# Input projections of the second token half in two 512-column chunks, with split weights reloaded from DRAM

## The chip, the cores and the metric

The kernel runs on one core of one Trainium2 chip. The metric is the device time of one execution in microseconds (us), as the median of several executions. Beside the timed executions one execution was profiled.

## The reference

One layer of a hybrid decoder. A token row is normalised, multiplied by one wide matrix, and its columns go to three branches; the branches are concatenated, multiplied by an output matrix, normalised and added to the input.

```python
xn = rmsnorm(x, g_pre)
proj = xn @ w_in                      # 1024 -> 4864 columns
a_c, b_c, g_c, x_r, g_r, q, g_q = jnp.split(proj, ...)   # 768 x5, 512 x2
u = a_c * sigmoid(b_c)
c = silu(layernorm(depthwise_causal(u, conv_w, conv_b))) * silu(g_c)   # 31 taps
xc = depthwise_causal(x_r, lru_conv_w, lru_conv_b)                     # 4 taps
h = linear_recurrence(a, bx_t, h0)    # a, bx_t from two small gate products of xc
rr = h * silu(g_r)
o = attention(q, mem_k, mem_v) * silu(g_q)              # 4 heads, 256 memory rows
y = x + rmsnorm(concatenate([c, rr, o]) @ w_out, g_post)
```

There are 2048 prompt tokens and 32 sample tokens (8 requests of 4) with caches of their own.

## The kernel before

Everything is float32. A product of two float32 matrices is made of three matmuls in a faster number format (`mm3`, L103): each operand is split into a high part that this format holds and the low rest, and high by high, high by low and low by high are added up in PSUM. `split` (L108) makes the two parts: ScalarE copies the high part (L109) and VectorE subtracts it from the source (L110).

**Two parts, then a phase 2.** In phase 1 the tokens are on the columns. Part 0 holds tokens 0 to 1023 and the 32 sample tokens, part 1 tokens 1024 to 2047; below they are called the first and the second part. Each part makes 38 projections, one per 128 output columns of `w_in` (six each for A, B, the conv gate GC, XR and GR, four each for Q and GQ). A projection (`proj`) loads its weight tile of 512 KB by a transfer on SyncE's queue (SP), splits it into `wh` and `wl`, and runs over the tokens in three chunks of 352, 352 and 320 columns (the last has 32 sample columns more in the first part); each chunk takes 8 contraction tiles of three matmuls. `wh`, `wl` have two buffers. The normalised x of a chunk stands in the tiles `xh`, `xl`, three buffers of 352 columns. In the second part x is loaded transposed and split by `split_cols` (ScalarE L356, VectorE L357).

Behind a projection stands an evacuation: for the conv gate a copy to `kc` and a store to DRAM (`store_mix`, L401), for A a ScalarE copy times 0.5 (L429) and a VectorE product, for GQ a silu. In `attn_o` the attention output is copied by ScalarE (L722) and multiplied by the gate on VectorE.

**What sets the order.** The string `ORDER` lists for each part which steps run when, with counts of chunks (G glu, X LRU input, S LRU scan, O LRU output, C conv gate, q and o attention); Tile's scheduler turns it into one instruction list for each engine. Every engine runs its list in order, and a transfer is issued by the engine on whose queue it stands: weight, x and cache loads on SP, all stores of phase 1 (`st_`) and a few reloads (`kv`, L663) on GpSimd (POOL). POOL also runs the `pow` of the norms and the three casts of each LRU gate chunk (L561 to L563, from `prep`), which wait for a VectorE split.

**Phase 2** multiplies blocks of 128 tokens by `w_out` in matmuls of 512 columns, after loading what phase 1 stored (`cr`, `mr`, L867 and L868).

Of the kernel before, what the change touches and what calls it, by code (L numbers as in the profile page):

```python
# [8 lines left out]
F32 = mybir.dt.float32  # L9
# [7 lines left out]
P = 128  # L17
# [15 lines left out]
EPS = 1e-6  # L33
CW = 352
CONV_LOW = 3000
MIX_HIGH = 500
# [3 lines left out]
NLC = 7  # L40
NCK = 5
NKC = 2
# [5 lines left out]
    "G0 N M1 X0:3 M0 X0:3 M2 X0:3 L X0 G1 G2:3 V G2 S0:2 S0:1 M3 S0:1 S0 C0 O0 C1 q0:3 G3:1 q0 G3 o0 R X1:7 X1 S1:1 G4 S1:1 S1:1 C2 C4 S1 O1 q1:3 G5:1 q1 G5:2 o1 G5 q3:3 C3:1 q3 C3 q2:3 o3:1 q2 o3 o2 C5",  # L48
    "G0:1 G0 s0 s1 p v0 X0 v1 G1 S0:1 G2:1 S0:1 G2 S0:1 S0 C0 O0 q0:3 G3:1 q0 G3:1 o0 G3 G4:3 X1 S1:1 G4 S1:1 S1 C1 O1 q1:3 G5:1 q1 G5 o1 q3:3 q2:1 q3 q2:2 o3:1 q2 o3 o2 C5 C4 C2 C3",
)  # L50
# [18 lines left out]
def hybrid_mixer_kernel(ctx, tc, x, xT, mem, consts, lnc, ccT, lcT, ckT, cv, w_in,  # L69
# [8 lines left out]
    convd = dram.tile([P, NT, TOK], F32, name="convd")  # L78
    rsd = dram.tile([1, TOK], F32, name="rsd")
    kvd = dram.tile([HEADS, P, 8, P], F32R, name="kvd")  # L80

# [13 lines left out]
    def bank(pl, w=512):  # L95
        t = pl.tile([P, 512], F32, tag="b", name="bk")
        return t[:, :w]
# [5 lines left out]
    def mm3(ps, lh, ll, rh, rl, first, last):  # L103
        pe.matmul(ps, lh, rh, start=first, stop=False)  # L104
        pe.matmul(ps, lh, rl, start=False, stop=False)  # L105
        pe.matmul(ps, ll, rh, start=False, stop=last)  # L106

    def split(hi, lo, src):  # L108
        act.activation(hi, src, AF.Copy)  # L109
        dve.tensor_tensor(lo, src, hi.bitcast(F32), op=ALU.subtract)  # L110

# [5 lines left out]
    def phase1():  # L117
        def pl_(name, bufs):
            return ctx1.enter_context(tc.tile_pool(name=name, bufs=bufs))
# [21 lines left out]
        def xslot(dt=F32):  # L141
            return pr.tile([P, XRW], dt, tag="xr", name="xr")
# [92 lines left out]

        def load_w(src, ahead=None):
            with tc.high_priority(offset=W_HIGH if ahead is None else ahead):
                raw = pw.tile([P, KD, P], F32, tag="wr", name="wr", bufs=WR)
                sp.dma_start(raw, src)
                wh = pw.tile([P, KD, P], F32R, tag="wh", name="wh")  # L240
                wl = pw.tile([P, KD, P], F32R, tag="wl", name="wl")
                split(wh, wl, raw)
            return wh, wl
# [53 lines left out]
        for part in range(2):  # L297
            chunks = []
            for c0 in range(0, PART, CW):
                n = min(CW, PART - c0)  # L300
                chunks.append((c0, n, SAMP if part == 0 and n < CW else 0))
            part_chunks.append(chunks)

        def pieces(part, c, r, w):
# [55 lines left out]
        for part in range(2):  # L360
            t0 = part * PART
            has_s = part == 0
            chunks = part_chunks[part]

            xh, xl = [], []
# [5 lines left out]
            ready[FIRST] = load_w(w_in[FIRST], 0)  # L371
            for c, (c0, n, ns) in enumerate(chunks):
                h = px.tile([P, KD, CW], F32R, tag="xh", name="xh")
                l = px.tile([P, KD, CW], F32R, tag="xl", name="xl")
                w = n + ns
                hi, lo = (lambda k: h[:, k, :w]), (lambda k: l[:, k, :w])
                if has_s:
                    if c + 1 < len(chunks):
                        rows[c + 1] = chunk_rows(0, c + 1)
                    if c == 0:  # L380
                        ready[M_A] = load_w(w_in[M_A], 0)
# [4 lines left out]
                xh.append(h)  # L386
                xl.append(l)
            def proj(m, evac):
                wh, wl = ready.pop(m) if m in ready else load_w(w_in[m])
                for c, (c0, n, ns) in enumerate(chunks):  # L390
                    w = n + ns
                    ps = bank(ps_p, w)
# [15 lines left out]
            def glu(i):  # L408
# [113 lines left out]
            def lru_scan(g):  # L522
# [13 lines left out]
                def prep(c):  # L536
                    c0, n, ns = chunks[c]
                    w = n + ns
# [30 lines left out]
                yield  # L569
                for c, (c0, n, ns) in enumerate(chunks):  # L570
                    w = n + ns
# [28 lines left out]
                    for i in range(3):  # L600
# [6 lines left out]
                        if ns:  # L607
# [5 lines left out]
                            dve.tensor_copy(xrb[i][1][:, :, :NS], hv)  # L613
                    if c + 1 < len(chunks):
                        nxt = prep(c + 1)
# [78 lines left out]
            def attn_o(h):  # L694
                kv, probs = att.pop(h)
                sg = {}

                def ev_g(c, ps):
                    c0, n, ns = chunks[c]
                    t = ck()  # L700
                    silu2(t[:, :n + ns], ps)
                    if ns:
                        act.activation(sgq[:, h, :], t[:, n:n + ns], AF.Copy)
                    sg[c] = t

                yield from proj(M_GQ + h, ev_g)
                ot = xslot()
                for q4 in range(2):
# [14 lines left out]
                for c, (c0, n, ns) in enumerate(chunks):  # L723
                    dve.scalar_tensor_tensor(ot[:, c0:c0 + n], ot[:, c0:c0 + n], 0.5, sg[c][:, :n],
                                             op0=ALU.mult, op1=ALU.mult)
                st_.dma_start(mixd[:, 2 * NT + h, t0:t0 + PART], ot[:, :PART])
# [63 lines left out]
            def conv_gate(i):  # L790
                def ev(c, ps):
                    c0, n, ns = chunks[c]
                    t = pk.tile([P, CW], F32, tag="kc", name="kc", bufs=NKC)[:, :n + ns]
# [266 lines left out]
```

## Time and profile before

| | us |
|---|---|
| median of 3 runs | 1429.61 (1429.36 to 1431.13) |
| profiled execution, its own time | 1426.34 |
| span in that profile, first to last instruction | 1424.6 |
| TensorE (PE) busy in the span | 1405.8 (99%) |
| VectorE (DVE) busy | 1096.5 (77%) |
| ScalarE (ACT) busy | 681.3 (48%) |
| GpSimd (POOL) busy | 152.0 (11%) |

The mean granted clock of TensorE is 0.997 of full speed. The span is 1.7 us shorter than the profiled execution's own time. The durations of one matmul overlap with the next, so the price of a matmul is the distance from its start to the next start, and not its own duration. In the profile PEld is TensorE's weight load, which overlaps PE. Idle time stands in the profile with what ended it.

### The profile page before, as it was taken

The page shows a single profiled execution, that of the slowest core. Times are in us where ns is not written, and L with a number is a line of the kernel's source. Part 1 is how long each engine was busy: PE and PEld are TensorE (multiplying, and loading weights), DVE is VectorE, ACT ScalarE, POOL GpSimd, SP SyncE. Part 2 cuts the span into 40 slices and gives each one's busy share as a digit, 9 for nine tenths or more (in the row PEclk, how much of TensorE's full clock was granted, in tenths as well). Part 3 has the DMA queues.
Part 4 walks back from the last instruction along what each step waited for, and adds up shares of the span by engine and source line. Part 5 has one row for each costly group of instructions (what it writes and reads, how often), then busy time and mean ns, then how long its engine had stood idle before and what let it go on. Part 6 is the DMA issues. An engine that isn't in the chain of part 4 may idle for free.

```text
span 1424.6 us, 21056 instructions
## 1 busy us (share of the span) xinstructions
PE 1405.8 (99%) x8376; PEld 1316.8 (92%) x8376; DVE 1096.5 (77%) x1481; ACT 681.3 (48%) x1326; POOL 152.0 (11%) x233
## 2 busy tenths in 40 slices
PE   9999999999999999999999999999999999999997
PEld 8999999999999999899999999999987788888885
DVE  7797985989889998699989996999874664545532
ACT  7524688346754344238833369434453442332421
POOL 2101121011210101011100110000100000000000
PEclk9999999999999999999999999999999999999998
DMA  6243416132261214621122311421474432423310
GB/s 220 80 83 119 129 64 232 46 93 76 81 191 52 91 65 151 226 88 51 55 89 67 97 49 57 164 88 42 142 250 130 137 118 85 141 93 118 126 60 30
DMA packets 97282, 152.24 MB, mean 107 GB/s; under 512 B 15224, under 2 KB 66800, under 8 KB 97184
## 3 DMA queue, kind: packets, MB, share of 16 engines
q1 hardware_dynamic: 84528, 118.66, 26.5%
q0 software_dynamic: 12656, 32.25, 6.7%
q8 instruction: 65, 1.06, 0.3%
q14 instruction: 33, 0.27, 0.1%
HBM read 114.84 MB, written 36.04 MB: 106 GB/s over the span
## 4 chain that ended last, share of the span: by engine, by line
PE 87%; ACT 5%; DMA 3%; DVE 2%; issue 2%; SPq 0%; POOL 0%; DVEq 0%; POOLq 0%; ACTq 0%
PE bk L104 28%; PE bk L106 28%; PE bk L105 28%; ACT lc L579 1%; PE bk L914 1%; PE bk L714 1%; DMA lc<-in_xT 1%; DVE wl L110 1%; ACT wh L109 1%; DMA big<-in_x 1%; ACT lc L588 0%; ACT lc L584 0%; PE bk L750 0%; DMA lc<-in_x 0%; DMA wr<-in_w_mem 0%
## 5 line engine op out<-in xcount | busy, mean ns | idle before, releaser
L104 PE MATMUL bk<-xh,wh 128*128 128x352 f32 (+1 forms) x1824 | 584.6, 322 | 1.3 <-ACT xh L232 0.7
L105 PE MATMUL bk<-xl,wh 128*128 128x352 f32 (+1 forms) x1824 | 583.6, 320 | 0.0
L106 PE MATMUL bk<-xh,wl 128*128 128x352 f32 (+1 forms) x1824 | 583.0, 321 | 0.4 <-DVE wl L110 0.4
L465 DVE SCALAR_TENSOR_TENSOR big<-ub,cst,big 128x1024 f32<-128x1024 f32 x360 | 457.6, 1283 | 8.9 <-issue 4.4
L104 PEld LDWEIGHTS bk<-xh,wh 128*128 128x128 f32 x1824 | 342.1, 188 | 4.0 <-issue 1.4
L105 PEld LDWEIGHTS bk<-xl,wh 128*128 128x128 f32 x1824 | 343.7, 188 | 1.5 <-issue 0.6
L106 PEld LDWEIGHTS bk<-xh,wl 128*128 128x128 f32 x1824 | 342.6, 188 | 2.1 <-issue 0.8
L105 PE MATMUL bk<-wol,mh 128*128 128x512 f32 x512 | 201.6, 394 | 1.3 <-DVE wol L110 1.3
L104 PE MATMUL bk<-woh,mh 128*128 128x512 f32 x512 | 200.3, 392 | 0.0
L106 PE MATMUL bk<-woh,ml 128*128 128x512 f32 x512 | 199.4, 391 | 0.0
L109 ACT ACTIVATE wh<-wr 128x1024 fp32r<-128x1024 f32 x84 | 89.0, 1059 | 125.6 <-PE bk L105 111.1
L110 DVE TENSOR_TENSOR wl<-wr,wh 128x1024 fp32r<-128x1024 f32 x84 | 103.5, 1232 | 29.1 <-ACT wh L109 24.4
L105 PEld LDWEIGHTS bk<-wol,mh 128*128 128x128 f32 x512 | 96.3, 188 | 20.3 <-DVE wol L110 1.8
L106 PEld LDWEIGHTS bk<-woh,ml 128*128 128x128 f32 x512 | 96.2, 188 | 19.8 <-issue 0.8
L104 PEld LDWEIGHTS bk<-woh,mh 128*128 128x128 f32 x512 | 96.2, 188 | 19.5
L891 ACT ACTIVATE cr<-cr,lnv 128x128 f32<-128x128 f32 (+1 forms) x102 | 40.7, 478 | 150.8 <-DVE cr L889 150.8
L579 ACT ACTIVATE lc<-bk,hb 128x352 f32<-128x352 f32 (+3 forms) x144 | 77.0, 545 | 26.3 <-PE bk L106 23.7
L552 DVE SCALAR_TENSOR_TENSOR lc<-xr,cst,lc 128x352 f32<-128x352 f32 (+2 forms) x126 | 60.4, 522 | 4.6 <-ACT lc L548 4.6
L889 DVE TENSOR_TENSOR cr<-cr,bk 128x768 f32<-128x768 f32 (+1 forms) x17 | 15.6, 918 | 57.1 <-PE bk L888 57.1
L931 DVE TENSOR_TENSOR o<-bk,gpb 128x512 f32<-128x512 f32 (+1 forms) x34 | 23.3, 686 | 32.3 <-ACT sqj L930 32.2
L930 ACT ACTIVATE sqj<-bk 128x512 f32<-128x512 f32 (+1 forms) x34 | 20.1, 592 | 46.0 <-PE bk L106 45.2
L894 DVE TENSOR_TENSOR cr<-cr,mr 128x768 f32<-128x768 f32 (+1 forms) x17 | 15.7, 923 | 32.2 <-ACT cr L891 32.2
(242 smaller groups left out, 1696.2 us busy)
## 6 DMA issues: line engine op xcount, KB each, us to landing
wr<-in_w_in SPq DMA_DIRECT2D x76, 512.0 KB, 3.8
mr<-mixd SPq DMA_DIRECT2D x16, 1024.0 KB, 5.6
raw<-in_w_out SPq DMA_DIRECT2D x16, 512.0 KB, 4.6
xt<-in_x SPq DMA_DIRECT2D x16, 512.0 KB, 5.4
out_y<-xt SPq DMA_DIRECT2D x15, 512.0 KB, 2.7
convd<-big POOLq DMA_DIRECT2D x12, 512.0 KB, 2.9
mixd<-big POOLq DMA_DIRECT2D x12, 512.0 KB, 6.1
cr<-convd SPq DMA_DIRECT2D x16, 384.0 KB, 4.9
```

Source lines behind the costliest of these rows:

```text
L104: pe.matmul(ps, lh, rh, start=first, stop=False)
L105: pe.matmul(ps, lh, rl, start=False, stop=False)
L106: pe.matmul(ps, ll, rh, start=False, stop=last)
L109: act.activation(hi, src, AF.Copy)
L110: dve.tensor_tensor(lo, src, hi.bitcast(F32), op=ALU.subtract)
L465: dve.scalar_tensor_tensor(acc[:, :PART], ub[:, j:j + PART], cw[:, i, j:j + 1], acc[:, :PART], op0=ALU.mult, op1=ALU.add)
L552: dve.scalar_tensor_tensor(o, src(j), lw[:, ch, j:j + 1], o, op0=ALU.mult, op1=ALU.add)
L579: act.activation(dst[lo_:hi_, i, :], ps[lo_:hi_, :], AF.Tanh, scale=0.5, bias=hb[lo_:hi_, a, 3 * g + i:3 * g + i + 1])
L891: act.activation(cr[:, i, :], cr[:, i, :], AF.Silu, scale=lng[:, i:i + 1], bias=lnb[:, i:i + 1])
L894: dve.tensor_tensor(cr, cr, mr[:, :NT, :m], op=ALU.mult)
L930: act.activation(sqj[:m, :], ps[n][:m, :], AF.Square, scale=float(D ** -0.5), accum_out=ms[:m, n:n + 1])
L931: dve.tensor_tensor(o[:m, ns], ps[n][:m, :], gpb[:m, ns], op=ALU.mult)
```

## The change

The x of a part now stands in one pair of tiles of 1056 columns. In the second part a projection runs in two chunks of 512 columns; the first part keeps its three. Steps that work on smaller pieces (the x split, the LRU gates) keep the chunks of 352, 352 and 320, called `subs`. In the first part each split weight pair is also stored to a DRAM tile `wd`, two transfers of 512 KB on POOL's queue; in the second part the pair is loaded from `wd`, again two transfers of 512 KB on POOL's queue, and nothing is split. The stores of the second part move to SP's queue. The 0.5 of A goes into its weights, so that its evacuation reads PSUM directly, and `attn_o` multiplies PSUM directly.

```diff
-NCK = 5
+NCK = 4
...
-        px = pl_("px", 3)
+        px = pl_("px", 1)
...
-    def split(hi, lo, src):
+    def split(hi, lo, src, scale=None):
...
+        def load_in(m, keep, ahead=None):
+            if keep:
+                wh, wl = load_w(w_in[m], ahead, 0.5 if M_A <= m < M_A + NT else None)
+                for i, t in enumerate((wh, wl)):
+                    pool.dma_start(wd[m, i], t.rearrange("p a b -> p (a b)"))
+            else:
+                wh = pw.tile([P, KD, P], F32R, tag="wh", name="wh")
+                wl = pw.tile([P, KD, P], F32R, tag="wl", name="wl")
+                for i, t in enumerate((wh, wl)):
+                    pool.dma_start(t.rearrange("p a b -> p (a b)"), wd[m, i])
+            return wh, wl
...
+        proj_chunks = [part_chunks[0], [(c0, PC, 0) for c0 in range(0, PART, PC)]]
+        xh = px.tile([P, KD, PART + SAMP], F32R, tag="xh", name="xh")
...
+            st_ = pool if has_s else sp
+            subs = part_chunks[part]
+            chunks = proj_chunks[part]
...
             def proj(m, evac):
-                wh, wl = ready.pop(m) if m in ready else load_w(w_in[m])
+                wh, wl = ready.pop(m) if m in ready else load_in(m, has_s)
...
-                        mm3(ps, wh[:, k, :], wl[:, k, :], xh[c][:, k, :w], xl[c][:, k, :w],
+                        mm3(ps, wh[:, k, :], wl[:, k, :], xh[:, k, cs], xl[:, k, cs],
...
                 def ev_a(c, ps):
-                    ah = ck()
-                    act.activation(ah[:, :ps.shape[1]], ps, AF.Copy, scale=0.5)
-                    for dst, src in parts(c, ah):
+                    for dst, src in parts(c, ps):
...
-                    act.activation(ot[:, q4 * 512:(q4 + 1) * 512], po, AF.Copy)
...
+                    dve.scalar_tensor_tensor(ot[:, os_], po, 0.5, ot[:, os_], op0=ALU.mult, op1=ALU.mult)
```

Counted over the whole kernel, matmuls of 352 columns go from 4800 to 2976, those of 320 from 960 to 48, those of 512 from 1746 to 3570: 912 matmuls fewer. VectorE loses the 38 weight splits of the second part, ScalarE these 38 copies, 36 copies of A and 16 of the attention output. POOL gets 76 stores and 76 loads of 512 KB and gives 36 stores to SP; SP loses 38 weight loads.

Three places in the instruction lists matter. First TensorE where the second part begins: in the rows, a name is output <- moving operand, weights; the bracket names the engine whose semaphore is waited for (DMASW: a transfer on POOL's queue, DMAHW: one on SP's). Before, the first projection of the second part (B, its bank bk_5631) follows the last of the first part (bk_5506):

```order
L106 MATMUL bk_5506<-xh_328,wl_5447 128x352
L104 MATMUL bk_5506<-xh_328,wh_5446 128x352
L105 MATMUL bk_5506<-xl_329,wh_5446 128x352
L106 MATMUL bk_5506<-xh_328,wl_5447 128x352
L104 MATMUL bk_5631<-xh_5542,wh_5538 128x352
L105 MATMUL bk_5631<-xl_5543,wh_5538 128x352 [waits DVE_49]
L106 MATMUL bk_5631<-xh_5542,wl_5539 128x352
```

Now the same place (bk_5519 is the last bank of the first part), and behind it the place a few rows on where the second projection (A, weights wh_5688 and wl_5689) begins:

```order
L108 MATMUL bk_5519<-xh_140,wl_5458 128x352
L106 MATMUL bk_5636<-xh_140,wh_5549 128x512 [waits DMASW3_49]
L107 MATMUL bk_5636<-xl_141,wh_5549 128x512 [waits DVE_49]
L108 MATMUL bk_5636<-xh_140,wl_5550 128x512 [waits DMASW4_49]
L106 MATMUL bk_5636<-xh_140,wh_5549 128x512
L106 MATMUL bk_5662<-xh_140,wh_5549 128x512 [waits Activation_49]
L107 MATMUL bk_5636<-xl_141,wh_5549 128x512 [waits DVE_49]
```

```order
L106 MATMUL bk_5692<-xh_140,wh_5688 128x512 [waits DMASW0_49]
L107 MATMUL bk_5422<-ptl_5407,kv_5023 128x512 [waits DVE_49]
L108 MATMUL bk_5636<-xh_140,wl_5550 128x512
L107 MATMUL bk_5692<-xl_141,wh_5688 128x512
L106 MATMUL bk_5718<-xh_140,wh_5688 128x512 [waits Activation_49]
L108 MATMUL bk_5692<-xh_140,wl_5689 128x512 [waits DMASW1_49]
```

TensorE now waits for the weight transfers themselves, no longer for a split, and a first chunk reads x columns that two pieces of the x split have written.

The second place is POOL's list inside the second part. Before, LRU casts (ck_6611, ck_6842) stand among stores:

```order
L561 CAST ck_6611<-lc_6595 128x352 [waits DVE_49,Pool_49]
L562 CAST ck_6611<-lc_6595 32x352 [waits Pool_49]
L563 CAST lc_6595<-lc_6595 32x352 [waits PE_49,Activation_49]
L401 DMA mixd_57<-kc_6943 128x352 [waits DMASW7_49,Activation_49]
L450 DMA out_nconvT<-ub_6496 128x30 [waits DMASW0_49,DVE_49]
L401 DMA mixd_57<-kc_6971 128x352 [waits DMASW1_49,Activation_49]
L401 DMA mixd_57<-kc_6999 128x320 [waits DMASW2_49,Activation_49]
L561 CAST ck_6842<-lc_6826 128x320 [waits DVE_49,PE_49,Pool_49]
```

Now the same kind of casts stand among the weight loads (wh, wl <- wd):

```order
L580 CAST ck_6288<-lc_6272 128x352 [waits DMAHW4_49,DVE_49]
L262 DMA wh_6297<-wd_60 128x1024 [waits DMASW5_49,DMASW2_49,PE_49]
L262 DMA wl_6298<-wd_60 128x1024 [waits DMASW6_49,PE_49]
L581 CAST ck_6288<-lc_6272 32x352 [waits Pool_49]
L582 CAST lc_6272<-lc_6272 32x352 [waits DMAHW3_49,Activation_49]
L262 DMA wh_6441<-wd_60 128x1024 [waits DMASW7_49,PE_49]
L262 DMA wl_6442<-wd_60 128x1024 [waits DMASW0_49,PE_49]
```

A load waits for TensorE to be done with the pair that held its buffer, and stands behind casts that wait for VectorE. What stood there before were stores.

The third place is the start of POOL's list. Before there are only the `pow` of the row norms; now the stores of the first two weight pairs stand between them:

```order
L221 TENSOR_TENSOR rs_196<-rs_196,mhalf_74 96x1 [waits DVE_49]
L257 DMA wd_60<-wh_151 128x1024 [waits Activation_49]
L257 DMA wd_60<-wl_152 128x1024 [waits DVE_49]
L221 TENSOR_TENSOR rs_263<-rs_263,mhalf_74 128x1 [waits DVE_49]
L221 TENSOR_TENSOR rs_270<-rs_270,mhalf_74 128x1 [waits DVE_49,Pool_49]
L257 DMA wd_60<-wh_165 128x1024 [waits Activation_49]
L221 TENSOR_TENSOR rs_277<-rs_277,mhalf_74 96x1 [waits DVE_49,Pool_49]
L257 DMA wd_60<-wl_166 128x1024 [waits DVE_49]
```

Four transfers of 512 KB begin while the x rows of the first part are still loaded.

## Rows read from the trace of the kernel before

**Rows 1.** The page: busy time, share of the span, instructions; then the chain by engine.

```profile
PE 1405.8 (99%) x8376; PEld 1316.8 (92%) x8376; DVE 1096.5 (77%) x1481; ACT 681.3 (48%) x1326; POOL 152.0 (11%) x233
...
PE 87%; ACT 5%; DMA 3%; DVE 2%; issue 2%; SPq 0%; POOL 0%; DVEq 0%; POOLq 0%; ACTq 0%
```

**Rows 2.** Windows: us of start and end, length, busy us per engine, clock, DMA, GB/s.

```profile
core 0: us, PE busy (x) PEld busy (x) DVE busy (x) ACT busy (x) POOL busy (x), PEclk, DMA share, GB/s
0.00:30.00 30.00, 27.55 (x183) 26.28 (x184) 22.59 (x83) 23.04 (x44) 8.01 (x20) 1.00 0.80 261
440.00:550.00 110.00, 110.00 (x704) 108.17 (x704) 104.82 (x141) 52.09 (x125) 11.50 (x19) 1.00 0.26 83
650.00:850.00 200.00, 200.00 (x1293) 199.34 (x1292) 187.61 (x223) 111.72 (x199) 25.10 (x31) 1.00 0.21 69
```

**Rows 3.** TensorE in time order, one projection's chunks of 352, 352, 320: start, duration.

```profile
701.59 0.32 PE L104 MATMUL bk<-xh,wh 128*128 128x352 f32 x1
...
709.27 0.31 PE L104 MATMUL bk<-xh,wh 128*128 128x320 f32 x1
...
712.79 0.32 PE L104 MATMUL bk<-xh,wh 128*128 128x352 f32 x1
```

**Rows 4.** TensorE in time order, matmuls of 512 columns in phase 2.

```profile
1035.27 0.40 PE L104 MATMUL bk<-woh,mh 128*128 128x512 f32 x1
...
1041.86 0.39 PE L106 MATMUL bk<-woh,ml 128*128 128x512 f32 x1
...
1201.03 0.39 PE L106 MATMUL bk<-woh,ml 128*128 128x512 f32 x1
...
1205.34 0.40 PE L104 MATMUL bk<-woh,mh 128*128 128x512 f32 x1
```

**Rows 5.** Groups by line: busy us, mean ns; idle before, releaser.

```profile
L109 ACT ACTIVATE wh<-wr 128x1024 fp32r<-128x1024 f32 x84 | 89.0, 1059 | 125.6 <-PE bk L105 111.1 <-DMA wr<-in_w_mem 7.3 <-issue 3.2
L110 DVE TENSOR_TENSOR wl<-wr,wh 128x1024 fp32r<-128x1024 f32 x84 | 103.5, 1232 | 29.1 <-ACT wh L109 24.4 <-PE bk L105 4.6
L429 ACT ACTIVATE ck<-bk 128x352 f32<-128x352 f32 (+1 forms) x36 | 16.2, 456 | 41.9 <-PE bk L106 41.8
L722 ACT ACTIVATE xr<-bk 128x512 f32<-128x512 f32 x16 | 9.5, 596 | 22.8 <-PE bk L106 22.7
```

**Rows 6.** The start: loads of the last x rows on SP, the first two weight splits.

```profile
5.44 3.75 SPq L204 DMA_DIRECT2D lc<-in_x  x4
...
8.86 1.07 ACT L109 ACTIVATE wh<-wr 128x1024 fp32r<-128x1024 f32 x1 [0.40 <-DMA wr<-in_w_in]
...
15.77 1.06 ACT L109 ACTIVATE wh<-wr 128x1024 fp32r<-128x1024 f32 x1
```

**Rows 7.** ScalarE where the second part begins: last evacuation before, first behind.

```profile
542.19 0.45 ACT L794 ACTIVATE kc<-bk 128x352 f32<-128x352 f32 x1
...
546.74 0.47 ACT L425 ACTIVATE ub<-bk 128x352 f32<-128x352 f32 x1
```

**Rows 8.** VectorE there: splits of the three x pieces.

```profile
532.03 1.57 DVE L357 SCALAR_TENSOR_TENSOR xl<-lc,cst,xh 128x352 fp32r<-128x352 f32 x3
...
541.49 2.07 DVE L357 SCALAR_TENSOR_TENSOR xl<-lc,cst,xh 128x352 fp32r<-128x352 f32 x4
...
546.54 1.07 DVE L357 SCALAR_TENSOR_TENSOR xl<-lc,cst,xh 128x352 fp32r<-128x352 f32 x2
...
548.66 1.93 DVE L357 SCALAR_TENSOR_TENSOR xl<-lc,cst,xh 128x320 fp32r<-128x320 f32 x4
...
553.07 1.00 DVE L357 SCALAR_TENSOR_TENSOR xl<-lc,cst,xh 128x320 fp32r<-128x320 f32 x2
```

**Rows 9.** Transfers: count, KB each, median us from issue to landing; POOL's issue.

```profile
wr<-in_w_in SPq DMA_DIRECT2D x76, 512.0 KB, 3.8
mr<-mixd SPq DMA_DIRECT2D x16, 1024.0 KB, 5.6
kv<-kvd POOLq DMA_DIRECT2D x8, 512.0 KB, 4.1
...
L663 POOL DMA_DIRECT2D kv<-kvd x8 | 4.3, 541 | 63.5 <-PE bk L106 63.3
```

**Rows 10.** The chain from phase 1 to phase 2: start us, us, what.

```profile
1035.52 0.45 ACT kc L794
1035.97 0.28 issue
1036.25 5.36 DMA mixd<-kc
1042.01 0.86 issue
```

**Rows 11.** Waits of POOL by line: us in total, times, longest.

```profile
POOL ck L561 <- DVE lc L110: 73.9, 7, 20.2
```

More of the change, by code (lines that the diff above doesn't have):

```diff
@@ L34 @@
 CW = 352
+PC = 512
 CONV_LOW = 3000
@@ L79, in hybrid_mixer_kernel @@
     rsd = dram.tile([1, TOK], F32, name="rsd")
+    wd = dram.tile([M_GQ + HEADS, 2, P, KD * P], F32R, name="wd")
     kvd = dram.tile([HEADS, P, 8, P], F32R, name="kvd")
@@ L106, in mm3 @@
         pe.matmul(ps, ll, rh, start=False, stop=last)
-    def split(hi, lo, src):
-        act.activation(hi, src, AF.Copy)
-        dve.tensor_tensor(lo, src, hi.bitcast(F32), op=ALU.subtract)
+    def split(hi, lo, src, scale=None):
+        if scale is None:
+            act.activation(hi, src, AF.Copy)
+            dve.tensor_tensor(lo, src, hi.bitcast(F32), op=ALU.subtract)
+        else:
+            act.activation(hi, src, AF.Copy, scale=scale)
+            dve.scalar_tensor_tensor(lo, src, scale, hi.bitcast(F32), op0=ALU.mult, op1=ALU.subtract)
     def silu2(o, src):
@@ L234, in transposed, with load_w @@
                                          op0=ALU.mult, op1=ALU.subtract)
-        def load_w(src, ahead=None):
+        def load_w(src, ahead=None, scale=None):
             with tc.high_priority(offset=W_HIGH if ahead is None else ahead):
@@ L241, in load_w @@
                 wl = pw.tile([P, KD, P], F32R, tag="wl", name="wl")
-                split(wh, wl, raw)
+                split(wh, wl, raw, scale)
+            return wh, wl
[4 more added lines that the diff above has]
+                    pool.dma_start(wd[m, i], t.rearrange("p a b -> p (a b)"))
+            else:
+                wh = pw.tile([P, KD, P], F32R, tag="wh", name="wh")
+                wl = pw.tile([P, KD, P], F32R, tag="wl", name="wl")
+                for i, t in enumerate((wh, wl)):
+                    pool.dma_start(t.rearrange("p a b -> p (a b)"), wd[m, i])
             return wh, wl
@@ L302, in phase1 @@
             part_chunks.append(chunks)
+        proj_chunks = [part_chunks[0], [(c0, PC, 0) for c0 in range(0, PART, PC)]]
+        xh = px.tile([P, KD, PART + SAMP], F32R, tag="xh", name="xh")
+        xl = px.tile([P, KD, PART + SAMP], F32R, tag="xl", name="xl")
         def pieces(part, c, r, w):
@@ L362, in phase1 @@
             has_s = part == 0
-            chunks = part_chunks[part]
-            xh, xl = [], []
+            st_ = pool if has_s else sp
+            subs = part_chunks[part]
+            chunks = proj_chunks[part]
             ready = {}
@@ L370, in phase1 @@
                 sp.dma_start(cst, consts)
[L371 to L376, printed above, removed]
+            ready[FIRST] = load_in(FIRST, has_s, 0)
+            for c, (c0, n, ns) in enumerate(subs):
+                cs = slice(c0, c0 + n + ns)
+                hi, lo = (lambda k: xh[:, k, cs]), (lambda k: xl[:, k, cs])
                 if has_s:
-                    if c + 1 < len(chunks):
+                    if c + 1 < len(subs):
                         rows[c + 1] = chunk_rows(0, c + 1)
                     if c == 0:
-                        ready[M_A] = load_w(w_in[M_A], 0)
+                        ready[M_A] = load_in(M_A, has_s, 0)
                     norm_rows(rows[c], xslot, KEEP if c == 0 else ())
@@ L385, in phase1 @@
                     split_cols(scaled_cols(part, c), gp, hi, lo)
-                xh.append(h)
-                xl.append(l)
             def proj(m, evac):
-                wh, wl = ready.pop(m) if m in ready else load_w(w_in[m])
+                wh, wl = ready.pop(m) if m in ready else load_in(m, has_s)
                 for c, (c0, n, ns) in enumerate(chunks):
-                    w = n + ns
-                    ps = bank(ps_p, w)
+                    cs = slice(c0, c0 + n + ns)
+                    ps = bank(ps_p, n + ns)
                     for k in range(KD):
-                        mm3(ps, wh[:, k, :], wl[:, k, :], xh[c][:, k, :w], xl[c][:, k, :w],
+                        mm3(ps, wh[:, k, :], wl[:, k, :], xh[:, k, cs], xl[:, k, cs],
                             k == 0, k == KD - 1)
@@ L536, in prep @@
                 def prep(c):
-                    c0, n, ns = chunks[c]
+                    c0, n, ns = subs[c]
                     w = n + ns
@@ L569, in lru_scan @@
                 yield
-                for c, (c0, n, ns) in enumerate(chunks):
+                for c, (c0, n, ns) in enumerate(subs):
                     w = n + ns
@@ L613, in lru_scan @@
                             dve.tensor_copy(xrb[i][1][:, :, :NS], hv)
-                    if c + 1 < len(chunks):
+                    if c + 1 < len(subs):
                         nxt = prep(c + 1)
@@ L695, in attn_o @@
                 kv, probs = att.pop(h)
-                sg = {}
+                ot = xslot()
                 def ev_g(c, ps):
                     c0, n, ns = chunks[c]
-                    t = ck()
-                    silu2(t[:, :n + ns], ps)
+                    silu2(ot[:, c0:c0 + n + ns], ps)
                     if ns:
-                        act.activation(sgq[:, h, :], t[:, n:n + ns], AF.Copy)
-                    sg[c] = t
+                        act.activation(sgq[:, h, :], ot[:, c0 + n:c0 + n + ns], AF.Copy)
                 yield from proj(M_GQ + h, ev_g)
-                ot = xslot()
                 for q4 in range(2):
@@ L721, in attn_o @@
                             mh == 0, mh == 1)
-                    act.activation(ot[:, q4 * 512:(q4 + 1) * 512], po, AF.Copy)
-                for c, (c0, n, ns) in enumerate(chunks):
-                    dve.scalar_tensor_tensor(ot[:, c0:c0 + n], ot[:, c0:c0 + n], 0.5, sg[c][:, :n],
-                                             op0=ALU.mult, op1=ALU.mult)
+                    os_ = slice(q4 * 512, (q4 + 1) * 512)
+                    dve.scalar_tensor_tensor(ot[:, os_], po, 0.5, ot[:, os_], op0=ALU.mult, op1=ALU.mult)
                 st_.dma_start(mixd[:, 2 * NT + h, t0:t0 + PART], ot[:, :PART])
@@ L792, in ev @@
                     c0, n, ns = chunks[c]
-                    t = pk.tile([P, CW], F32, tag="kc", name="kc", bufs=NKC)[:, :n + ns]
+                    t = pk.tile([P, PC], F32, tag="kc", name="kc", bufs=NKC)[:, :n + ns]
                     act.activation(t, ps, AF.Copy)
```

2 lines of the change are left out of this document (1 added, 1 removed).

## The prediction

> **What bounds the kernel now.** I read the page first. TensorE is busy 99% of the span and has 87% of the chain of waits; VectorE is at 77% [rows 1]. The windows then say whether that average holds where the change works: in a stretch of the first part and in one of the second TensorE is busy for the whole window, 110.00 of 110 us and 200.00 of 200 us, while VectorE is at 95% and 94% and the transfers at a quarter or less [rows 2]. So in both parts TensorE's stream sets the time, and an edit counts in two ways only: it shortens that stream, or it makes the stream wait. VectorE is close behind as the next bound. Last I read TensorE in time order for the price of one matmul, start to next start.
>
> **What the stream loses.** One projection of the second part is now 48 matmuls of 352 columns in 709.27 - 701.59 = 7.68 us (160.0 ns each) and 24 of 320 in 712.79 - 709.27 = 3.52 us (146.7 ns): 11.20 us [rows 3]. After the change it is 48 matmuls of 512. Phase 2 has that shape: 19 in 1205.34 - 1201.03 = 4.31 us, 226.8 ns each, so 48 take 10.89 us; in another stretch 29 take 1041.86 - 1035.27 = 6.59 us, 227.2 ns, so 10.91 us [rows 4]. The columns are the same in both cases; what goes is a cost per matmul. From the first two shapes, 160.0 and 146.7 ns for 32 columns more or less, a column costs 0.416 ns and a matmul some 13.5 ns beside its columns; 512 columns give 226.6 ns by that line, as the phase 2 rows do. The saving is 0.31 us a projection (0.29 by the other stretch), times 38: **-11.8 us**, at least -11.1.
>
> The Trainium skill, "TensorE: Matmul & The Clock Gate", section "Wait — 56ns, not 53.3ns?", gives a warm matmul only about 2.5 ns beside its columns; by that the 912 matmuls fewer would save 912 x 2.5 = 2.3 us. The trace disagrees (13.5 ns), and the trace decides.
>
> **What the other engines lose.** 38 splits on ScalarE (1059 ns) and VectorE (1232 ns), 36 copies of A (456 ns) and 16 of the attention output (596 ns) [rows 5]: some 66 us of ScalarE and 47 us of VectorE. I cost this at nothing. The cover is TensorE's full window; as these engines are not waited for there, their time buys none. It does give VectorE, at 94% of the second window, some slack, which makes every wait on it less likely.
>
> **The traffic.** 76 stores of 0.5 MB in the first part, over some 500 us, are about 80 GB/s on top of 83 with the transfers 26% busy [rows 2]; in the second part a pair is 1 MB in place of 0.5. Both hide, except in three places.
>
> - **Start.** Four stores of 512 KB fall among the first x rows, where the transfers are 80% busy at 261 GB/s [rows 2]. At that rate 2 MB are 8 us, if all of it pushed the x rows back and nothing lay between; at the other end it is nothing, since TensorE works on chunk 0 of two projections meanwhile. TensorE loses 2.45 of the first 30 us now [rows 2]. The last x rows of the part are issued from 5.44 on, and the first weight is split only at 8.86, the second at 15.77 [rows 6]; a store follows its split, so most of the 8 us falls behind the x rows: I take **+1.5**, 0 to 8.
> - **Where the second part begins.** TensorE leaves the first part just ahead of the copy at 542.19, and now is done with the first 352 columns of B before 546.74 [rows 7]. In the new order the first chunk needs 512 columns, that is the second piece of the x split too, and VectorE does that at 541.49 to about 547.6; the third piece runs from 548.66 to about 554.1 [rows 8]. A chunk of 24 takes 24 x 0.2268 = 5.4 us. Its eight contraction tiles are wanted from about 542 on, 0.7 us apart, and the splits come at 542.0 to 547.6: up to 1 us late. The second chunk wants the third piece from 548 to 553: 1 to 1.5 us late. Second, A's weight pair can be loaded only when the last matmul of the first part has freed its buffer. Two issues of 0.54 us and a landing of 4.1 to 5.6 us [rows 9] make 5.2 to 6.7 us, and only the 5.4 us of B's first chunk and the attention matmuls among it lie between. The waits overlap: **+2**, 0 to 8 (1 + 1.5 + 1.3 one behind the other, plus the 4.1 us of one more landing).
> - **Inside the second part** a pair is called for when the pair two projections back is done, so it has one projection, 10.9 us, to be issued (2 x 0.54) and to land (4.1; the 1 MB row says 5.6 [rows 9]): a slack of 4.2 to 5.7 us. Small misses, mostly where the cache loads of the sample tokens run beside: **+1**, 0 to 4 without the rival below.
>
> The end of phase 1 changes little: the last `kc` store already stands in the chain for 5.36 us [rows 10] behind phase 2 matmuls, and is now 256 KB from SP in place of 160 KB from POOL. At 261 GB/s the 96 KB more are 0.4 us; against it stands one store less queued. I take 0, within 1 each way.
>
> **Sum:** -11.8 + 1.5 + 2 + 1 + 0 = -7.3 us. The profiled execution, 1426.34 us, would become 1419.0. It lies 3.3 us below the median of the runs, 1429.61; I apply the difference to the median: **1422.3 us**.
>
> **Rivals.** A difference under 0.2%, 2.9 us, can't be told from no change.
>
> *Weights late behind casts (slower).* In the second part POOL's list puts six groups of LRU casts among the loads; seven such waits took 73.9 us before, 10.6 each [rows 11], behind which only stores stood. If one holds the queue for 10.6 us after the buffer is free, TensorE waits 10.6 less the slack of about 5, so 5.6 us, six times 34 us: 1422 + 34 = 1456. It decides when the six waits together cost over 7.3 us, that is when a cast holds the queue for about 6.2 us after the release. For it: the casts wait for VectorE, the next bound. Against it: these waits of 10.6 us were measured on an otherwise idle POOL, from the time it arrived and not from the time at which a weight was due; TensorE waits for the same LRU chunks in its own list and lost nothing in 200 us [rows 2]; and VectorE is relieved by 47 us.
>
> *POOL's transfers starved by VectorE (slower).* If POOL could write a transfer's descriptors only while VectorE is idle, 12.4 of 200 us [rows 2], the 1.08 us of two issues would need 17 us of each 10.9 us projection, 6 us late, 38 times: some 230 us more. Against it: the `kv` loads on POOL's queue land in 4.1 us, the weights on SP's in 3.8, and an issue takes 541 ns [rows 9]. The Trainium skill, "SBUF — State Buffer", section "SBUF: two separate sides", warns of such a starvation of GpSimd's queue while VectorE runs a two-port operation; these rows show none of it.
>
> *Gain eaten (same).* The start at 6 us and the border at 5: -11.8 + 6 + 5 + 1 = +0.2, 1429.8. For it: both places put a transfer ahead of TensorE that had cover before. Against it: at the start the x rows are issued ahead of the stores [rows 6].
>
> *The change does not shorten the stream (same or slower).* If 512 columns of `wh` by `xh` cost what 352 do per column, 160.0/352 x 512 = 232.7 ns, a projection is 11.17 us and the saving 1.1 us; with the costs 1433. Against it: the phase 2 rows, the same engine with the same kind of operands [rows 4].
>
> **How the numbers follow.** Forecast 0.72; late weights 0.11; starved queue 0.02; gain eaten 0.12; no shorter stream 0.03. The forecast's own range is 1417 (all costs at nothing: 1417.8, and less if VectorE's relief is worth a little) to 1426. To leave out no more than 2 in 10, I go up through the eaten gain: 1416.5 to 1430.5. Faster takes the forecast and a little of the eaten gain, 0.73; same takes the rest of that and the missing saving, 0.14; slower the two rivals of the queue, 0.13.
>
> **What the changed profile would show.** Right: matmuls of 512 columns 226 to 228 ns apart in the second part, 48 to a projection; TensorE full in a window of 200 us there; ScalarE some 66 us and VectorE 47 us less busy; weight loads landing in 4 to 6 us with waits for TensorE ahead of them. A wait of a few us at the border and little at the start. Wrong: gaps on TensorE ahead of the first matmul of a projection, put down to a load of `wh` or `wl`, with POOL waiting at a cast just before; x rows of the second and third chunk later by several us in the first 50; or a spacing above 230 ns.

## The result, and the profile after

The changed kernel takes **1442.34 us** (1439.42 to 1444.95), against 1429.61 before: 1.0085 times as long by the means of the runs, 95% interval 1.0071 to 1.0100. Forecast were 1422.3 us, 1416.5 to 1430.5. It is slower by 12.7 us where 7.3 less were expected: 20 us apart. The span of the profiled execution went from 1424.6 to 1437.6 us.

Page of the changed kernel: busy time; chain by engine; transfers with KB each and median us from issue to landing.

```profile
PE 1410.1 (98%) x7464; PEld 1236.5 (86%) x7464; DVE 1054.5 (73%) x1409; ACT 618.9 (43%) x1204; POOL 200.8 (14%) x337
...
PE 84%; DVE 6%; DMA 6%; ACT 2%; issue 2%; SPq 0%; DVEq 0%; POOLq 0%; ACTq 0%
...
wr<-in_w_in SPq DMA_DIRECT2D x38, 512.0 KB, 5.6
wd<-wh POOLq DMA_DIRECT2D x38, 512.0 KB, 3.2
wd<-wl POOLq DMA_DIRECT2D x38, 512.0 KB, 6.3
wh<-wd POOLq DMA_DIRECT2D x38, 512.0 KB, 3.6
wl<-wd POOLq DMA_DIRECT2D x38, 512.0 KB, 4.5
```

Against [rows 1] ScalarE (681.3 to 618.9) and VectorE (1096.5 to 1054.5) lost 62.4 and 42.0 us where 66 and 47 were forecast, and the chain has 6% of transfers and of VectorE where it had 3% and 2%. The weights' own load on SP's queue now takes 5.6 us and not 3.8 [rows 9].

Windows of the changed kernel, the first three as in [rows 2], then one across the border of the parts, then two places where TensorE now waits.

```profile
core 0: us, PE busy (x) PEld busy (x) DVE busy (x) ACT busy (x) POOL busy (x), PEclk, DMA share, GB/s
0.00:30.00 30.00, 24.30 (x152) 22.36 (x152) 18.49 (x70) 20.71 (x38) 10.68 (x24) 0.94 0.98 330
440.00:550.00 110.00, 110.00 (x705) 108.50 (x704) 103.51 (x139) 49.48 (x127) 17.52 (x31) 1.00 0.45 142
650.00:850.00 200.00, 200.00 (x915) 165.27 (x914) 176.64 (x200) 92.80 (x165) 26.83 (x42) 1.00 0.32 107
...
545.00:575.00 30.00, 30.00 (x145) 25.23 (x144) 25.96 (x36) 8.67 (x18) 6.85 (x12) 1.00 0.45 146
...
240.00:244.00 4.00, 3.94 (x28) 3.57 (x27) 1.36 (x8) 2.98 (x7) 1.65 (x4) 1.00 1.06 407
244.00:248.00 4.00, 1.01 (x7) 0.81 (x5) 1.92 (x3) 3.27 (x7) 1.99 (x4) 0.87 1.05 417
248.00:252.00 4.00, 4.00 (x17) 3.94 (x16) 2.83 (x8) 1.80 (x8) 1.30 (x1) 0.50 1.06 411
252.00:256.00 4.00, 4.00 (x21) 4.00 (x21) 2.47 (x7) 4.00 (x14) 0.00 (x0) 0.77 0.47 167
...
1080.00:1084.00 4.00, 1.33 (x8) 1.02 (x6) 2.19 (x5) 4.00 (x14) 0.00 (x0) 0.91 0.00 0
1084.00:1088.00 4.00, 3.99 (x10) 2.16 (x11) 3.54 (x7) 0.72 (x1) 1.20 (x1) 0.50 0.91 256
```

Read the four rows from 240 to 256 together. At 244 the transfers run at 417 GB/s and all their time is taken; TensorE works 1.01 of 4 us. In the next row it is busy throughout but at a granted clock of 0.50, its lower level of 1.2 GHz, and does 17 matmuls where the row of 240 held 28; from 252 the mean is still 0.77. So this wait of 3 us cost about twice its length: at half the clock some 2.0 us more are lost in the row of 248, and 0.9 in that of 252. The last two rows show the same at another place. The chain of waits says what was late there (start us, us, what):

```profile
234.91 0.20 ACT lc L350
235.11 0.02 issue
235.13 10.46 DMA lc<-in_x
245.59 0.02 issue
245.61 0.02 ACTq L350
245.63 0.32 issue
245.95 1.15 ACT lc L350 x2
247.10 0.36 ACT xr L691
247.46 0.04 issue
247.50 0.58 PE bk L106
```

`lc<-in_x` are rows of the second part, whose norms `part_stats` computes on ScalarE (L350). One load took 10.46 us beside a pair's stores. ScalarE runs its list in order, so the evacuation of an attention query (`xr`, L691) stood behind it, and TensorE waited for that. TensorE's waits by line, us in total, times, longest:

```profile
PE bk L106 <- ACT xr L691: 4.6, 2, 3.0
PE bk L106 <- ACT xh L238: 3.9, 2, 2.5
PE bk L928 <- DVE mh L113: 2.7, 1, 2.7
PE bk L764 <- DMA ks<-in_ckT: 1.9, 1, 1.9
```

The second is the x split at the start, the third the sample block of phase 2, the fourth a load of the sample cache. No wait is for a load of `wh` or `wl`.

Last, the price of a matmul in the changed kernel: 95 matmuls of 512 columns in a row in the second part, first and last.

```profile
719.68 0.40 PE L107 MATMUL bk<-xl,wh 128*128 128x512 f32 x1
...
741.50 0.40 PE L108 MATMUL bk<-xh,wl 128*128 128x512 f32 x1
```

21.82 us for 94 steps are 232.1 ns, and not the 226.8 of [rows 4]. The kernel before had shown that price, where I did not look: its `mem_v` in the first part has 12 matmuls of 512 columns in a row,

```profile
125.90 0.40 PE L104 MATMUL bk<-wh,lc 128*128 128x512 f32 x1
...
128.45 0.39 PE L106 MATMUL bk<-wh,lc 128*128 128x512 f32 x1
```

11 steps in 2.55 us, 231.8 ns.

**Where the time went.** Both kernels multiply the same number of columns, so two traces can be laid side by side by work done: for each point of the kernel before, the columns of TensorE's matmuls (those of 256 columns or more) up to there, and the time at which another kernel has done as many. The table gives what each kernel lost (+) or won in each stretch of the kernel before, worked out so from the traces; the others are the experiments below.

| stretch of before, us | changed | two chunks only | stores only | reloads only | changed, x rows of 1024 |
|---|---|---|---|---|---|
| 0 to 30 | +4.7 | +1.5 | +5.6 | +1.6 | +5.6 |
| 30 to 225 | -0.9 | -1.4 | -0.6 | -1.7 | -0.8 |
| 225 to 250 | +5.1 | +0.8 | +4.9 | +0.4 | +3.6 |
| 250 to 550 | +0.5 | +1.1 | +1.3 | +4.7 | +6.9 |
| 550 to 650 | +2.9 | -0.1 | +2.3 | -0.1 | -1.4 |
| 650 to 1025 | -3.5 | -3.5 | -3.5 | -3.5 | -9.2 |
| 1025 to 1050 | -2.0 | +3.5 | +4.7 | -2.0 | -2.2 |
| 1050 to 1400 | +6.2 | 0.0 | +0.1 | +5.0 | +5.0 |

Of the 3.5 us won from 650 to 1025, 0.7 is a wait that the kernel before has near 892 us. A single profiled execution stands behind each column; stretches differ by a microsecond or two between kernels that are equal there, and from 250 to 550 by more: 6.4 us between the changed kernel and the one with x rows of 1024, whose code is the same there. In that execution TensorE worked 0.18 of 4 us from 432 to 436, beside transfers at 376 GB/s, and the clock behind it was 0.60; the changed kernel's own trace has 3.51 us and 1.00 there.

### The profile page after: what moved, and what is told of

It reads as the page before. It is cut to its first block, busy times and chain, and to the rows that moved or that the text cites. A ratio compares the mean times of both kernels' runs of the same rounds, so it can differ in the third digit from the quotient of the medians.

```text
span 1437.6 us, 19216 instructions
## 1 busy us (share of the span) xinstructions
PE 1410.1 (98%) x7464; PEld 1236.5 (86%) x7464; DVE 1054.5 (73%) x1409; ACT 618.9 (43%) x1204; POOL 200.8 (14%) x337
## 4 chain that ended last, share of the span: by engine, by line
PE 84%; DVE 6%; DMA 6%; ACT 2%; issue 2%; SPq 0%; DVEq 0%; POOLq 0%; ACTq 0%
PE bk L108 27%; PE bk L107 27%; PE bk L106 27%; DVE big L484 2%; PE bk L928 1%; DMA ck<-in_ccT 1%; PE bk L730 1%; DMA lc<-in_mem 1%; DVE lc L571 1%; DMA ks<-in_ckT 1%; DVE wl L113 1%; DMA lc<-in_x 1%; DMA big<-in_x 1%; DMA lc<-in_xT 1%; DMA wr<-in_w_mem 0%
## 5 line engine op out<-in xcount | busy, mean ns | idle before, releaser
L106 PE MATMUL bk<-xh,wh 128*128 128x352 f32 (+1 forms) x1520 | 534.9, 353 | 3.9 <-ACT xh L238 3.9
L107 PE MATMUL bk<-xl,wh 128*128 128x352 f32 (+1 forms) x1520 | 535.7, 353 | 0.0
L108 PE MATMUL bk<-xh,wl 128*128 128x352 f32 (+1 forms) x1520 | 533.3, 352 | 0.0
L106 PEld LDWEIGHTS bk<-xh,wh 128*128 128x128 f32 x1520 | 286.1, 188 | 31.8 <-ACT xh L238 4.4
L107 PEld LDWEIGHTS bk<-xl,wh 128*128 128x128 f32 x1520 | 286.6, 189 | 25.9 <-issue 0.8
L108 PEld LDWEIGHTS bk<-xh,wl 128*128 128x128 f32 x1520 | 286.3, 189 | 25.8 <-issue 0.8
L598 ACT ACTIVATE lc<-bk,hb 128x352 f32<-128x352 f32 (+2 forms) x144 | 77.4, 545 | 39.7 <-PE bk L108 37.3
L112 ACT ACTIVATE wh<-wr 128x1024 fp32r<-128x1024 f32 x40 | 42.3, 1058 | 92.0 <-PE bk L107 73.2
L113 DVE TENSOR_TENSOR wl<-wr,wh 128x1024 fp32r<-128x1024 f32 x40 | 49.4, 1235 | 13.3 <-ACT wh L112 8.5
L257 POOL DMA_DIRECT2D wd<-wh x38 | 20.7, 545 | 226.8 <-ACT wh L112 164.5
```

Source lines behind the costliest of these rows:

```text
L257: pool.dma_start(wd[m, i], t.rearrange("p a b -> p (a b)"))
L598: act.activation(dst[lo_:hi_, i, :], ps[lo_:hi_, :], AF.Tanh, scale=0.5, bias=hb[lo_:hi_, a, 3 * g + i:3 * g + i + 1])
```

## The experiments

**The place of the operands.** My first idea for 232 against 227 ns was the place in SBUF: all tiles of phase 1 began 32 bytes off a multiple of 64, those of phase 2 on one. A tile of 32 bytes ahead of phase 1 moves them.

```diff
+        shift = pl_("shift", 1).tile([P, 8], F32, name="shift")
+        pool.memset(shift, 0.0)
         pl = pl_("pl", NLC)
```

> The changed kernel with all tiles of phase 1 moved up by 32 bytes in each partition, so that x, weights and attention operands begin on multiples of 64 bytes, as phase 2's tiles do. Theory A (the place of the operands in SBUF sets the price of a 512-column matmul: 232 ns in phase 1, 227 ns in phase 2): the 512-column matmuls of the second part fall to about 227 ns, 38 x 48 x 5 ns = 9 us less, some 1433 us median; those of 352 columns unknown, 160 ns or a little less. Theory B (what the other engines do in phase 1 sets it): they stay at 232 ns and the time at 1442 us within 2 us.

Measured: 1444.71 us, 1.0105 (1.0089 to 1.0122) of before; this interval overlaps the changed kernel's. The 512-column matmuls of the second part have a mean distance of 231.9 ns, as in the changed kernel. The idea in this form falls.

> The kernel before with the same shift by 32 bytes. Theory A: its few 512-column matmuls of phase 1 fall from 232 to 227 ns, well under 1 us in all; whether 352 and 320 columns (160.3 and 146.5 ns) fall too isn't known from any row: 0 to 5 ns each, so 0 to 25 us less. Theory B: no change, 1430 us within 2 us.

Measured: 1429.35 us, 1.0001 (0.9991 to 1.0010). No change.

**The two chunks alone.** Every weight is loaded raw and split, in both parts.

```diff
         def load_in(m, keep, ahead=None):
...
-                    pool.dma_start(wd[m, i], t.rearrange("p a b -> p (a b)"))
...
-                    pool.dma_start(t.rearrange("p a b -> p (a b)"), wd[m, i])
+            return load_w(w_in[m], ahead, 0.5 if M_A <= m < M_A + NT else None)
...
-            st_ = pool if has_s else sp
+            st_ = pool
```

> The two chunks of 512 alone: both parts load and split their weights as before, nothing goes to DRAM and back, and the second part's stores stay on GpSimd's queue. My theory (the traffic of the split weights makes the stalls at the start, near 245 us, near 600 us and at the start of phase 2, and the 512-column matmuls at 232 ns save only 2.3 us): 1425 to 1430 us. Rival (the stalls come from the larger chunks and the single x tile): 1436 us or more.

Measured: 1428.83 us, 0.9995 (0.9986 to 1.0003). On balance the chunks cost nothing and win nothing; the 13 us come with the traffic and the stores moved to SP. The windows show it at the place of the 10.46 us load: TensorE is full, at the full clock, and the transfers take a quarter of their time.

```profile
244.00:248.00 4.00, 4.00 (x27) 4.00 (x26) 2.09 (x7) 3.37 (x15) 0.00 (x0) 1.00 0.24 90
248.00:252.00 4.00, 4.00 (x27) 4.00 (x26) 3.21 (x5) 4.00 (x9) 0.00 (x0) 1.00 0.00 0
```

> The two chunks alone, and the shift by 32 bytes. If theory A and the traffic theory hold, both savings add up: 9 to 10 us below the two chunks alone, 1416 to 1420 us, below the kernel before. If the price of a matmul doesn't follow the place of its operands, as the two chunks alone.

Measured: 1428.18 us, 0.9995 (0.9986 to 1.0004), as the two chunks alone. The traffic idea held, the shift again did nothing.

**Stores or reloads.** The changed kernel with one half of the traffic each. Stores only, in the second part:

```diff
-                for i, t in enumerate((wh, wl)):
-                    pool.dma_start(t.rearrange("p a b -> p (a b)"), wd[m, i])
+                wh, wl = load_w(w_in[m], ahead, 0.5 if M_A <= m < M_A + NT else None)
...
-            st_ = pool if has_s else sp
+            st_ = pool
```

> The first part stores all 76 split tiles, but nobody reads them: the second part loads and splits its weights raw, in two chunks of 512, and its stores stay on GpSimd's queue. Theory (the stores collide with the x rows at the start and with the row loads near 245 us, each stall followed by a stretch at the half clock): the start costs 3 to 4 us more than in the kernel before, the stretch near 245 us 5 us, the end of phase 1 as in the two chunks alone; 1436 to 1439 us. Rival (the reloads and the moved stores make the loss): within 2 us of the two chunks alone, 1429 us.

Measured: 1439.11 us, 1.0071 (1.0052 to 1.0090). The same stall, with the same clock behind it:

```profile
244.00:248.00 4.00, 1.51 (x13) 1.31 (x11) 1.30 (x2) 3.12 (x5) 1.63 (x3) 0.98 1.06 416
248.00:252.00 4.00, 3.48 (x14) 3.42 (x15) 3.52 (x9) 1.60 (x7) 2.21 (x2) 0.50 1.04 410
```

Reloads only:

```diff
-                for i, t in enumerate((wh, wl)):
-                    pool.dma_start(wd[m, i], t.rearrange("p a b -> p (a b)"))
+                if m == M_GC:
+                    for i, t in enumerate((wh, wl)):
+                        pool.dma_start(wd[0, i], t.rearrange("p a b -> p (a b)"))
...
-                    pool.dma_start(t.rearrange("p a b -> p (a b)"), wd[m, i])
+                    pool.dma_start(t.rearrange("p a b -> p (a b)"), wd[0, i])
```

> One weight pair is stored in the first part, and every projection of the second part loads this one pair (so it multiplies by the wrong weights; only the time is of use); the second part's stores stand on SP's queue as in the changed kernel. Theory: the first part costs nothing more than in the two chunks alone; the second part loses some 2 us near 575 us to the loads of the sample cache and 4 to 6 us at the start of phase 2, where the sample block's load stands behind stores on SP; 1433 to 1437 us. Rival (stores make all of the loss): 1429 us.

Measured: 1430.36 us, 1.0007 (0.9996 to 1.0018). So the stores make some 10 us of the loss (1439.11 against 1428.83), the reloads and the moved stores 1 to 2. I had given the reloads 4 to 8. Near 575 nothing is lost. The loss in phase 2 is there, 5.0 us behind 1050, at one wait for the sample block (`mh`), as in the changed kernel; the two chunks alone have none of it. They lose 3.5 us before 1050 instead, waiting for the split of a `w_out` tile (`wol`), where reloads only wins 2.0. So little of it is left in the time. The two waits, in the two chunks alone and in reloads only:

```profile
PE bk L106 <- DVE wol L112: 4.5, 2, 2.4
...
PE bk L929 <- DVE mh L113: 2.7, 1, 2.7
```

**What makes a matmul of 512 columns cost 232 ns.** Two edits to the two chunks alone take over one property of phase 2 each. First, three matmuls into one bank and three into the next:

```diff
+                    pss = [bank(ps_p, n) for _, n, _ in chunks]
+                    for k in range(KD):
+                        for ps, (c0, n, _) in zip(pss, chunks):
+                            cs = slice(c0, c0 + n)
+                            mm3(ps, wh[:, k, :], wl[:, k, :], xh[:, k, cs], xl[:, k, cs],
+                                k == 0, k == KD - 1)
...
```

> The two chunks alone, but a projection of the second part runs both chunks at once, three matmuls into one PSUM bank and three into the other in turn, as phase 2 does. If the row of 24 matmuls into one bank makes them 232 ns: 227 ns and 9 us less than the two chunks alone, some 1420 us. If not: 232 ns, 1429 us, or 1 to 3 us more since a bank's evacuation comes later.

Measured: 1435.69 us, 1.0048 (1.0029 to 1.0066). The mean distance is 231.0 ns; the banks are not it. It takes 7 us longer, more than the 1 to 3 that I gave; both evacuations now come at a projection's end, but that they are the reason was not taken apart.

Second, x rows of 1024 columns in the second part, so that a contraction tile begins 4096 bytes after the last and not 4224; the projections and the x split use `xv` and `xw` in place of `xh` and `xl`:

```diff
+            def packed(t):
+                if has_s:
+                    return t
+                return t.rearrange("p a b -> p (a b)")[:, :KD * PART].rearrange("p (a b) -> p a b", a=KD)
+            xv, xw = packed(xh), packed(xl)
```

> The two chunks alone, but in the second part x stands in rows of 1024 columns in the same tile, so that each contraction tile begins 4096 bytes on (as phase 2's moving operand), and not 4224. If the pitch of the moving operand makes the matmuls 232 ns, which differ between even and odd contraction tiles by 2 ns now: 227 ns without that difference, 9 us less than the two chunks alone apart from a few us at the border of the parts. If not: 232 ns, 1429 to 1433 us.

Measured: **1421.26 us, 0.9946 (0.9932 to 0.9961)**: faster than both kernels. 72 matmuls in a row of its second part, first and last:

```profile
729.91 0.40 PE L105 MATMUL bk<-xh,wh 128*128 128x512 f32 x1
...
746.04 0.40 PE L107 MATMUL bk<-xh,wl 128*128 128x512 f32 x1
```

16.13 us for 71 steps: 227.2 ns, the price of [rows 4]. Over all its 512-column projections the mean is 227.7, against 231.9 in the two chunks alone.

The same with another pitch:

```diff
-                return t.rearrange("p a b -> p (a b)")[:, :KD * PART].rearrange("p (a b) -> p a b", a=KD)
+                return t.rearrange("p a b -> p (a b)")[:, :KD * (PART + 16)].rearrange("p (a b) -> p a b", a=KD)
```

> The two chunks alone with x in rows of 1040 columns, 4160 bytes, in the second part. If it is the pitch that counts, and not how the second part's x lies against the first's: 230 to 233 ns for a 512-column matmul, as with 1056 columns. If any tighter layout does: 227 ns.

Measured, in a single execution: 1428.77 us, and a mean of 231.8 ns. The same 72 matmuls, first and last:

```profile
733.33 0.40 PE L105 MATMUL bk<-xh,wh 128*128 128x512 f32 x1
...
749.78 0.39 PE L107 MATMUL bk<-xh,wl 128*128 128x512 f32 x1
```

16.45 us for 71 steps: 231.7 ns. Rows of 4160 bytes cost what rows of 4224 cost; with 4096 the price falls. Of the three pitches tried, 4096 alone is cheap.

And the rows of 1024 columns in the changed kernel itself, by the same `packed`:

> The changed kernel with one edit: in the second part x stands in rows of 1024 columns. If the price of the 512-column matmul was the larger half of my error: 227 to 228 ns, some 8 us less than the changed kernel, 1433 to 1435 us, still above the kernel before by the 4 to 6 us that the traffic costs beyond what was forecast. If the reloads of weights become the bound once the stream is shorter: 1438 us or more.

Measured: 1429.78 us, 1.0010 (0.9996 to 1.0024), with 227.8 ns: 12.6 us below the changed kernel (10.7 by the two ratios), more than the 8 expected. In the stretch from 650 to 1025 its trace wins 9.2 us in place of 3.5, which is 5.7 of it for most of the projections; its profiled execution took 1433.99 us, above the median of 1429.78, so the rest can't be placed.

**Which stores.** The changed kernel without the first two pairs' stores and without the two near 245 us; these four are loaded raw and split again in the second part.

```diff
+                if len(asked) in (0, 1, 15, 16):
+                    skipped.add(m)
+                asked.append(m)
+            if keep or m in skipped:
                 wh, wl = load_w(w_in[m], ahead, 0.5 if M_A <= m < M_A + NT else None)
+                for i, t in enumerate((wh, wl) if m not in skipped else ()):
...
```

> The changed kernel, but four of the 38 weight pairs are not stored and are loaded raw and split again in the second part: the first two (the start) and the two whose stores run beside the row loads near 245 us. If these stores make the two stalls: 3 us less lost at the start and 4 to 5 us less near 245 us, 1434 to 1436 us. If any traffic of this size does, whichever pair it is: 1440 us or more.

Measured: 1437.70 us, 1.0060 (1.0046 to 1.0074), between the two forecasts. By work done it is 0.9 us behind the kernel before at 30 us, where the changed kernel is 4.7, and it loses 2.4 us from 225 to 250 where that loses 5.1. Both places respond to just these stores:

```profile
20.00:30.00 10.00, 9.54 (x67) 9.12 (x66) 9.65 (x36) 8.36 (x19) 3.79 (x5) 1.00 0.63 181
244.00:248.00 4.00, 3.80 (x25) 3.80 (x26) 2.97 (x8) 1.66 (x7) 0.00 (x0) 1.00 0.49 135
```

Of the 6.5 us saved there the time keeps 4.6; its trace loses 6.2 us from 550 to 575, against 1.5 in the changed kernel: its waits for the sample cache's load are 3.8 us, against 1.9, and the clock is 0.50 from 574 to 578.

**The start of phase 2.** With short rows and no traffic the gain up to 1025 us is 10 us, and 5.2 are lost right behind it: TensorE works 1.39 of 4 us from 1032 to 1036, and the clock of the next two stretches of 4 us is 0.52 and 0.62. The last conv gate in the old chunks was to bring them back.

```diff
+                mine = subs if i == 3 else chunks
...
-                yield from proj(M_GC + i, ev)
+                yield from proj(M_GC + i, ev, mine)
```

> The two chunks alone with x in rows of 1024 columns, and the last conv gate of the second part in chunks of 352, 352 and 320, as in the kernel before, so that its last store is the short one again. If the 5 us that the two chunks lose at the start of phase 2 come from the long last chunk: 1416 to 1418 us, 4 to 5 us below the same kernel with a long last chunk. If they come from elsewhere (the block loads, the scheduler's order): 1421 us.

Measured: 1421.29 us, 0.9945 (0.9932 to 0.9957), as with a long last chunk. The idea falls.

## Why the prediction was wrong, point by point

**The price of the stream: wrong, about half of the error.** The step "Phase 2 has that shape" took 226.8 ns from [rows 4] and carried it to other operands. The second part's x stands in rows of 4224 bytes, and there it is 232.1 ns: a projection takes 48 x 0.2321 = 11.14 us, 0.06 less than before, 2.3 us for 38 and not 11.8. Shown by one edit: rows of 4096 bytes give 227.2 ns and 7.6 us. Of the 20 us between forecast and result, 9.5 are this step; 9.0 are the traffic, forecast at 1.5 + 2 + 1 and measured at 13.5 between the two chunks alone and the changed kernel. The rival "the change does not shorten the stream" had the price (232.7 ns) and a chance of 0.03; its counterargument, the phase 2 rows, was the mistake. The Trainium skill's 2.5 ns beside a matmul's columns ("TensorE: Matmul & The Clock Gate", "Wait — 56ns, not 53.3ns?") would also have given 2.3 us; the trace disagrees with how it comes there, as the 13.5 ns are there and are saved where the pitch is right.

**"Both hide, except in three places": wrong.** 38 MB of stores were averaged over 500 us. They come in pairs of 1 MB, and beside a pair the transfers reach 417 GB/s and one row load 10.46 us, where the median of these loads was 5.4 us before. The place near 245, 5.1 us, was none of my three. By medians the stores cost 10 us, shown by taking them alone, the reloads and the moved stores together 1 to 2.

**The start: mechanism right, size off.** Forecast +1.5, measured +4.7, of which the two chunks alone have 1.5 and the first two pairs' stores about 3.8 (4.7 against 0.9). It lay within the 0 to 8 that I gave.

**The border of the parts: wrong by 2.** The second part begins at 550.09 in the changed kernel, and TensorE is busy for 30.00 of 30 us from 545 to 575; no wait was left to pay.

**Late weights, starved queue: rightly held unlikely.** No wait of TensorE names a weight load; they land in 3.6 and 4.5 us on GpSimd's queue while VectorE is busy for 176.64 of 200 us. The slack of 4 to 6 us was enough (with x rows of 1024 one wait of 0.4 us for such a load appears). The +1 for small misses can't be checked alone: from 550 to 650 the changed kernel loses 2.9, 1.9 of it a wait for a cache load, but stores only loses 2.3 there and reloads only nothing.

**The end of phase 1, taken as 0: wrong by 4, and at another place.** From 1025 to 1050 the changed kernel wins 2.0 us. It loses 6.2 behind that, at one wait of 2.7 us for the sample block of phase 2 and at the lower clock behind it. All five kernels that reload weights and store on SP's queue have this wait of 2.7 us; none of the others has it. So it came with the reloads or the moved stores, which were not taken apart. The two chunks alone lose their 3.5 us at the other wait, before 1050: in their chain the next block's load (`cr<-convd`) takes 6.92 us from 1037.86 and stands ahead of VectorE's split of a `w_out` tile. A short last chunk doesn't mend it. What holds that load back was not isolated and stays open.

**What no step had:** the clock. Behind the wait near 245 us TensorE stood at 1.2 GHz (0.50 from 248 to 252), and likewise behind the wait at 1081 us (0.50 from 1084 to 1088); at the start the mean is 0.71 from 16 to 20 us, behind 4 us in which it worked 2.33. The two chunks alone have that too (0.68 behind 2.37 us of work), the kernel before has not (1.00 behind 2.90). I priced waits at their length. Over the whole profiled execution the mean granted clock is 0.992, against 0.997 before; in the timed executions it is 0.990 to 0.993, against 0.994 and more before. From that an estimate: 0.005 of 1437.6 us are some 7 us, at most, of the 12.7, since part of the low stretches is idle time. Not every wait is followed by it: in the two chunks alone TensorE works 1.56 and 1.91 of 4 us from 1040 to 1048, and the clock stays at 1.00.

## What to carry to other kernels

Take the price of an operation from rows with the same operands in the same layout, not only of the same shape: between two places with "the same" matmul the distance from one row of the moving operand to the next was worth 5 ns in 227, which is 9 us over the 38 projections and more than the forecast gain of 7.3. Traffic that hides on average must be laid against the bursts beside which it falls, above all against loads for which an in-order engine waits. And splitting a weight again on engines that TensorE doesn't wait for was cheaper than keeping the result in DRAM: the same chunks with x rows of 4096 bytes run at 0.9946 of the kernel before without the traffic, and at 1.0010 with it.

## What the runs showed of the hardware

- Matmuls of 512 columns whose moving operand lies in rows of 4096 bytes are 227.2 ns apart; 4224 or 4160 bytes, 232. In the two chunks alone the means by operand pair and by even or odd contraction tile go from about 231 to 234 ns; with 4096 bytes they lie between 227.5 and 228. A shift of everything by 32 bytes (tried with 4224) changes nothing, the order of the banks 1 ns at most. It isn't the whole rule: the attention and `mem_v` matmuls, whose moving operands begin 2048 bytes apart, stay at 231 ns beside the fast ones. Matmuls of 352 columns (160 ns) showed no difference between rows of 1408 and 4224 bytes.
- The price did not follow the other engines: in the two chunks alone it is 231.9 ns in stretches without any transfer and 232.0 where the transfers are over 60% busy, and 232 where VectorE is busy for under 30% as where it is for over 90% (means over stretches of 2 us).
- Of a pair's two stores of 512 KB on one queue the first lands in 3.2 us, the second in 6.3 (medians of 38).
